# A diffusion block's opening: another order of loads, one unit beside the modulations, one behind them, and filler matmuls

## The chip, the cores and the metric

The kernel runs on one core of one Trainium2 chip. The metric is the device time of one execution in microseconds (us), the median of the runs shown. Activations lie transposed in the core: 128 partitions hold features, the free axis holds the tokens. There are 256 latent tokens (LAT) and 256 context tokens (CTX), so a row of both is 512 columns wide, and 1024 features are eight chunks of 128, called k below.

## The reference, cut to what matters

The model has two layers. Each layer computes nine modulation vectors per stream from a conditioning vector, then an FFN branch, a mixer and a second FFN branch. Only the start of the first layer matters here:

```python
mod  = split(silu(c)     @ ada_w[0] + ada_b[0], 9)
modc = split(silu(c_ctx) @ ada_w[0] + ada_b[0], 9)

def ffn_branch(h, g, shift, scale, gate, w13, w2):
    a = rmsnorm(h, g) * (1.0 + scale) + shift
    g_, up = split(a @ w13, 2)
    return 0.5 * gate * ((silu(g_) * up) @ w2)

h  = h  + ffn_branch(h,  norm_g[0, 0], mod[0],  mod[1],  mod[2],  ffn_w13[0, 0], ffn_w2[0, 0])
hc = hc + ffn_branch(hc, norm_g[0, 0], modc[0], modc[1], modc[2], ffn_w13[0, 0], ffn_w2[0, 0])
```

The first product with w13 needs the normed and modulated activations, and these need shift and scale of both streams, that is 8 MB of ada_w, and the mean squares of both streams.

## The kernel before

**Precision.** A product of float32 is made of three matmuls. An operand is split into a high part in the chip's fp32r type and a low part, the difference: a_h and a_l for activations, wh and wl for weights, g_h and g_l for the FFN's inner activations. `mm3` issues wh by a_h, wh by a_l and wl by a_h for each chunk k.

**Units.** The weights come in units of 1 MB, a pair of 128-column blocks: for w13 one gate block and one up block. `Units.fetch` issues the load on SP's queue into a raw tile (two buffers), `Units.load` splits it: ScalarE copies to wh, VectorE subtracts to wl, once per block. wh and wl have five buffers each. `units.get` hands a unit out and loads the next. A whole unit of w13 takes 48 matmuls of 512 columns: two blocks, eight chunks, three matmuls.

**Modulations.** For the first norm the shifts and scales are computed on TensorE in four quads of 1 MB twice (`quad_load`, kh 0 and 1). `quad_sum` runs 16 small matmuls for each half (32 rows in the profile, since a float32 matmul shows as two rows), which add into a PSUM tile gt. `quad_end` copies gt to gs on VectorE (L118), transposes it on TensorE (L119) and makes mod (L122) and gain (L124) on VectorE for two chunks k. Quad q serves the chunks 2q and 2q+1.

**Norm.** `rstd_diag` sums squares over the partitions with matmuls (st), makes the mean (L244), takes the power -1/2 on GpSimd (L246) and builds diagonal matrices (L249). `rstd_rows` broadcasts them with a matmul (bc). `norm_k` makes for one chunk and one stream u on VectorE (L261), a_h on ScalarE (L264) and a_l on VectorE (L265). u has three buffers.

**Opening.** `first` loads, in the program's order, quad 0, unit 0, quad 1, unit 1, quads 2 and 3; all `adaq` tiles share four buffers, so quads 2 and 3 wait until quad 0's and 1's sums have read theirs. The squares of h (L997, L999, L1003), 20 warming matmuls on ones into a tile called warm, the statistics, quad 0 and the first two norms follow. `pair` then computes units 0 and 1 together: for chunks 0 to 5 it issues both units' matmuls of the chunk and calls the hook ahead of chunks 0, 2 and 4, which sums quads 1, 2 and 3 and makes their norms; chunks 6 and 7 close the two units, and `glu` makes g_h and g_l. Then unit 2 and the rest follow, one unit after the other.

**What sets the order.** The tile framework plans the order of each engine's instructions itself, by the program's order and by when it expects operands and buffers. Three things bind it: data and buffer dependences; `keep_in_program_order`, which `MM` uses while the list `in_order` holds something, so that these TensorE instructions keep the order of the program; and `issue_after(ins)`, which puts the instructions traced in its block behind `ins` on the engine of `ins` alone. Before, the pinned stretch ends ahead of quad 0's end; the order of the tiles and sums behind it is the planner's. All large loads go through SP's queue, four small ones through ScalarE's.

Of the kernel before, what the change touches and what calls it, by code (L numbers as in the profile page):

```python
# [10 lines left out]
F32 = mybir.dt.float32  # L11
F32R = mybir.dt.float32r
# [37 lines left out]
def hybrid_block(ctx: ExitStack, tc: tile.TileContext, h_in, s_in, s_row, ada0, ada, ada_b, norm_g, final_g,  # L50
# [17 lines left out]
    def ps_t(shape, name):  # L68
        return ps.tile(shape, F32, tag="t", name=name, bufs=2)
# [1 line left out]
    h = big.tile([P, KD, NT], F32, name="h")  # L71
    a_h = Rows(big.tile([P, KD * NT + P], F32R, name="a_h"))
    a_l = Rows(big.tile([P, KD * NT + P], F32R, name="a_l"))
    g_h = big.tile([P, KD, NT], F32R, name="g_h")
    g_l = big.tile([P, KD, NT], F32R, name="g_l")
    A = (a_h, a_l)
    GG = (g_h, g_l)

    sv = const.tile([P, KD, 32], F32, name="sv")
    nc.scalar.dma_start(out=sv, in_=s_in)  # L80
    for hf in BOTH:
        nc.sync.dma_start(out=h[:, :, HALF[hf]], in_=h_in[hf])
    ab = const.tile([P, 2, 9, KD, 2], F32, name="ab")
    nc.scalar.dma_start(out=ab, in_=ada_b)
    ng = const.tile([P, 2, 3, KD, 2], F32, name="ng")
# [16 lines left out]
    def quad_load(pool, q):  # L102
        us = []
        for kh in range(2):
            u = pool.tile([P, 4, 512], F32, tag="adaw", name=f"adaq{q}_{kh}", bufs=4)
            nc.sync.dma_start(out=u, in_=ada0[q, kh])
            us.append(u)
        return us

    def quad_sum(gt, kh, u):  # L110
        for kc in range(4):
# [4 lines left out]
    def quad_end(pool, gt, q):  # L116
        gs = pool.tile([P, P], F32, tag="gs", name=f"gs{q}", bufs=2)
        V.tensor_copy(out=gs, in_=gt[:, 0, :])  # L118
        T.transpose(out=gt[:, 1, :], in_=gs, identity=ident)  # L119
        k = slice(2 * q, 2 * q + 2)  # L120
        src = gt[:, 1, :].rearrange("p (k m c) -> p k m c", k=2, m=2)[:, :, :, 0:2]
        V.tensor_tensor(out=mod[0][:, 0:2, k, :].rearrange("p m k r -> p k m r"), in0=src,  # L122
                        in1=ab[:, 0, 0:2, k, :].rearrange("p m k r -> p k m r"), op=ALU.add)
        V.scalar_tensor_tensor(out=gain[0][:, 0, k, :], in0=mod[0][:, 1, k, :], scalar=1.0, in1=ng[:, 0, 0, k, :],  # L124
                               op0=ALU.add, op1=ALU.mult)
# [131 lines left out]
    def norm_k(li, n, hf, bc, k):  # L257
        tag = f"n{li}_{n}_{hf}_{k}"
        sh = mod[li][:, 3 * n, k, hf:hf + 1]
        u = tmp.tile([P, NL], F32, tag="u", name=f"u_{tag}", bufs=3)  # L260
        V.scalar_tensor_tensor(out=u, in0=h[:, k, HALF[hf]], scalar=gain[li][:, n, k, hf:hf + 1], in1=bc,  # L261
                               op0=ALU.mult, op1=ALU.mult)
        ah = a_h[:, k, HALF[hf]]
        S.activation(out=ah, in_=u, func=AF.Identity, bias=sh)  # L264
        V.scalar_tensor_tensor(out=a_l[:, k, HALF[hf]], in0=u, scalar=sh, in1=ah.bitcast(F32),  # L265
                               op0=ALU.add, op1=ALU.subtract)

    def norm_begin(li, n, hf):
        dg = rstd_diag(ssq[hf], D, f"n{li}_{n}_{hf}")
# [98 lines left out]
    def ffn(li, fi, halves, items, nxt, first=None):  # L368
# [3 lines left out]
        with tc.tile_pool(name=f"ffn{f}", bufs=2) as fp:  # L372
# [20 lines left out]
            def pair(ws, cols, nm, nouter, hook=None):  # L393
# [9 lines left out]
                for j in range(2):  # L403
                    for x in range(2):
                        mm3(accs[j][x], ws[j][x], A, range(nouter, KD), cols, first=(nouter == 0))
                    glu(accs[j][0], accs[j][1], j, cols, f"{tag}_{j}_{nm}")

            def raw_glu(pg, pu, j, bc, nm):

                sh = fp.tile([P, 2], F32, tag="sh", name=f"sh_{nm}")  # L410
                ts = []
                for x, pp in enumerate((pg, pu)):
                    V.tensor_copy(out=sh[:, x:x + 1], in_=pp[:, NL:NL + 1])
                    ts.append(fp.tile([P, NL], F32, tag=f"t{x}", name=f"t{x}_{nm}"))
# [24 lines left out]
            if len(halves) == 1:  # L439
                bc = raw_pair()  # L440
            elif first:
                hook = first(fp)
                ws = [units.get(f"{tag}u{j}") for j in range(2)]
                pair(ws, slice(0, NT), "a", 6, hook)
# [4 lines left out]
            if prep:  # L449
                prep()  # L450
            slot()
            slot()
# [532 lines left out]
    ffn_units(3, (LAT,))  # L985

    def first(fp):
        qs = [quad_load(fp, 0)]
        pins = units.load()
        qs.append(quad_load(fp, 1))  # L990
        units.load()
        qs += [quad_load(fp, 2), quad_load(fp, 3)]
        for hf in BOTH:
            sq = []
            for x in range(4):
                sq.append(fp.tile([P, 2, NL], F32, tag="sg" if x < 2 else "gg", name=f"sq_{hf}_{x}"))
                S.activation(out=sq[x], in_=h[:, 2 * x:2 * x + 2, HALF[hf]], func=AF.Square)  # L997
                if x % 2:
                    V.tensor_tensor(out=sq[x - 1], in0=sq[x - 1], in1=sq[x], op=ALU.add)  # L999
            ssq[hf] = [tmp.tile([P, NL], F32, tag=f"ssq{hf}", name=f"ssq{hf}_in", bufs=1),  # L1000
                       tmp.tile([P, NL], F32, tag="sq", name=f"sq{hf}_in", bufs=2)]
            for x in range(2):
                V.tensor_tensor(out=ssq[hf][x], in0=sq[0][:, x, :], in1=sq[2][:, x, :], op=ALU.add)  # L1003
        gt = ps_t([P, 2, P], "gt0")
        wm = acc([P, NT], "warm")
        in_order.append(1)
        for _ in range(20):
            MM(wm[:, 0:P], ones, ones, start=True, stop=True)
        dgs = [rstd_diag(ssq[LAT], D, "n0_0_0")]
        quad_sum(gt, 0, qs[0][0])  # L1010
        bcs = [rstd_rows(dgs[0], "n0_0_0")]
        dgs.append(rstd_diag(ssq[CTX], D, "n0_0_1"))
        quad_sum(gt, 1, qs[0][1])
        bcs.append(rstd_rows(dgs[1], "n0_0_1"))
        in_order.clear()
        quad_end(fp, gt, 0)

        def norms(q):
            if q:
                gt = ps_t([P, 2, P], f"gt{q}")  # L1020
                for kh in range(2):
                    quad_sum(gt, kh, qs[q][kh])
                quad_end(fp, gt, q)
            for k in (2 * q, 2 * q + 1):
                for hf in BOTH:
                    norm_k(0, 0, hf, bcs[hf], k)
        with tc.issue_after(pins[0].ins), tc.issue_after(pins[1].ins):
            norms(0)
        return lambda k: norms(k // 2 + 1) if k in (0, 2, 4) else None

    ffn(0, 0, BOTH, [(0, m, kp, 2) for m in range(2, 8) for kp in range(4)], (0, 1), first)
    na_layer(0)
# [111 lines left out]
```

## Time and profile before

| | us |
|---|---|
| median of 3 runs | 1791.26 |
| lowest, highest | 1790.46, 1792.51 |
| profiled execution | 1788.52 |
| its span, first to last instruction | 1786.4 |
| TensorE busy in it | 1761.5 |
| granted TensorE clock, mean | 0.995 |

The span is one execution seen by the hardware profiler; the execution's own time holds 2.1 us more around it. A granted clock of 1.00 is 2.4 GHz and one of 0.50 is 1.2 GHz. In the rows PE is TensorE, PEld its weight loads, DVE VectorE, ACT ScalarE, POOL GpSimd, and SPq the queue of SP. A row that says "x3" merges three instructions in a row, and its second number runs from the start of the first to the end of the last.

### The profile page before, as it was taken

Reading aid. Unit: us, or ns where it says so; the run is one execution under the profiler, and the core shown is the slowest. Engines: PE = TensorE matmul, PEld = TensorE weight load, DVE = VectorE, ACT = ScalarE, POOL = GpSimd, SP = SyncE. Lnnn points to the kernel's source line nnn. Section 1 sums busy time; section 2 is a strip of 40 time slices with the busy share of each in tenths; the row PEclk is TensorE's granted clock in tenths of the full one; section 3 lists DMA queues with packets and bytes.
Section 4 is the critical chain, followed back from the end, with each engine's and each line's share of the span. In section 5 each row is a group of like instructions: output and inputs, shape, how many; then the busy total and the mean of one; then the engine's idle time right before and its main releaser. Section 6 shows DMA issues by size and latency. Waiting matters only on the chain.

```text
span 1786.4 us, 24670 instructions
## 1 busy us (share of the span) xinstructions
PE 1761.5 (99%) x9920; PEld 1520.3 (85%) x9920; DVE 1181.2 (66%) x2042; ACT 699.5 (39%) x1074; POOL 23.4 (1%) x42
## 2 busy tenths in 40 slices
PE   7999999999999999999999999999999999999998
PEld 6888888897777798888888988888889988999997
DVE  4897777366678778877773666553335776677665
ACT  3422213235455543222223332221223856654443
POOL 0000000000000000000000000000000000000000
PEclk8999999999999999999999999999999999999999
DMA  9665552322131235645543255532222422245542
GB/s 388 229 234 185 196 189 94 105 97 101 36 113 65 81 118 194 230 165 190 195 153 145 95 181 212 196 142 94 95 94 95 154 71 72 95 160 195 177 180 93
DMA packets 42834, 263.70 MB, mean 148 GB/s; under 512 B 4960, under 2 KB 7392, under 8 KB 13152
## 3 DMA queue, kind: packets, MB, share of 16 engines
q1 hardware_dynamic: 40128, 257.97, 39.6%
q10 hardware_dynamic: 2592, 4.16, 0.8%
q8 instruction: 78, 1.28, 0.3%
q14 instruction: 36, 0.29, 0.0%
HBM read 261.06 MB, written 1.05 MB: 147 GB/s over the span
## 4 chain that ended last, share of the span: by engine, by line
PE 96%; ACT 1%; DVE 1%; DMA 1%; issue 0%; POOL 0%; SPq 0%; POOLq 0%; DVEq 0%; ACTq 0%
PE pu_f L200 22%; PE pg_f L200 22%; PE po_f2g L200 5%; PE po_f0g L200 5%; PE po_f1g L200 5%; PE pkq L200 5%; PE po_f3g L200 4%; PE nav_p L200 2%; PE mlv_p L200 2%; PE mpk L200 2%; PE pat L200 1%; PE sp L200 1%; PE mpq L200 1%; PE po_mlwo L200 1%; PE po_nao L200 1%; PE mpo L200 1%
## 5 line engine op out<-in xcount | busy, mean ns | idle before, releaser
L140 DVE SCALAR_TENSOR_TENSOR jk<-ada,sb 128x1024 f32<-128x1024 f32 x224 | 273.6, 1221 | 3.5
L388 DVE TENSOR_TENSOR gg_f<-sg_f,pu_f 128x512 f32<-128x512 f32 x60 | 41.2, 687 | 154.7 <-PE pu_f L200 154.7
L180 ACT ACTIVATE wh_f2u<-raw_f2u 128x1024 fp32r<-128x1024 f32 x44 | 46.7, 1062 | 148.2 <-PE pg_f L200 55.3
L180 ACT ACTIVATE wh_f1u<-raw_f1u 128x1024 fp32r<-128x1024 f32 x44 | 46.7, 1062 | 142.4 <-PE pg_f L200 51.8
L180 ACT ACTIVATE wh_f0u<-raw_f0u 128x1024 fp32r<-128x1024 f32 x44 | 46.4, 1060 | 135.2 <-PE pg_f L200 50.3
L181 DVE TENSOR_TENSOR wl_f2u<-raw_f2u,wh_f2u 128x1024 fp32r<-128x1024 f32 x44 | 53.9, 1224 | 39.0 <-ACT wh_f2u L180 37.8
L180 ACT ACTIVATE wh_f3u<-raw_f3u 128x1024 fp32r<-128x1024 f32 x44 | 46.1, 1058 | 48.5 <-PE pg_f L200 15.9
L181 DVE TENSOR_TENSOR wl_f1u<-raw_f1u,wh_f1u 128x1024 fp32r<-128x1024 f32 x44 | 53.8, 1224 | 16.3 <-ACT wh_f1u L180 15.2
L181 DVE TENSOR_TENSOR wl_f0u<-raw_f0u,wh_f0u 128x1024 fp32r<-128x1024 f32 x44 | 53.7, 1223 | 15.0 <-ACT wh_f0u L180 14.0
L181 DVE TENSOR_TENSOR wl_f3u<-raw_f3u,wh_f3u 128x1024 fp32r<-128x1024 f32 x44 | 53.4, 1222 | 13.5 <-ACT wh_f3u L180 13.4
L200 PE MATMUL pg_f<-a_h,wh_f1u 128*128 128x512 f32 x160 | 62.3, 389 | 0.0
L200 PE MATMUL pg_f<-a_h,wh_f2u 128*128 128x512 f32 x160 | 62.3, 389 | 0.0
L200 PE MATMUL pg_f<-a_l,wh_f1u 128*128 128x512 f32 x160 | 62.3, 389 | 0.0
L200 PE MATMUL pg_f<-a_l,wh_f2u 128*128 128x512 f32 x160 | 62.3, 389 | 0.0
L200 PE MATMUL pg_f<-a_h,wh_f0u 128*128 128x512 f32 x160 | 62.2, 389 | 0.0
L200 PE MATMUL pg_f<-a_l,wh_f0u 128*128 128x512 f32 x160 | 62.2, 389 | 0.0
L200 PE MATMUL pg_f<-a_h,wl_f0u 128*128 128x512 f32 x160 | 62.2, 389 | 0.0
L200 PE MATMUL pu_f<-a_h,wh_f0u 128*128 128x512 f32 x160 | 62.2, 389 | 0.0
L200 PE MATMUL pu_f<-a_l,wh_f0u 128*128 128x512 f32 x160 | 62.2, 389 | 0.0
L200 PE MATMUL pu_f<-a_h,wl_f0u 128*128 128x512 f32 x160 | 62.2, 389 | 0.0
L200 PE MATMUL pg_f<-a_h,wl_f1u 128*128 128x512 f32 x160 | 62.2, 389 | 0.0
L200 PE MATMUL pu_f<-a_h,wh_f1u 128*128 128x512 f32 x160 | 62.2, 389 | 0.0
(509 smaller groups left out, 5617.4 us busy)
## 6 DMA issues: line engine op xcount, KB each, us to landing
ada<-in_ada SPq DMA_DIRECT2D x64, 1024.0 KB, 5.6
raw_f0u<-in_w SPq DMA_DIRECT2D x22, 1024.0 KB, 4.9
raw_f1u<-in_w SPq DMA_DIRECT2D x22, 1024.0 KB, 4.9
raw_f2u<-in_w SPq DMA_DIRECT2D x22, 1024.0 KB, 4.8
raw_f3u<-in_w SPq DMA_DIRECT2D x22, 1024.0 KB, 4.8
adaq<-in_ada SPq DMA_DIRECT2D x8, 1024.0 KB, 12.4
raw_f0g<-in_w SPq DMA_DIRECT2D x8, 1024.0 KB, 4.8
raw_kq<-in_na_kq SPq DMA_DIRECT2D x8, 1024.0 KB, 4.8
```

The source lines that it names most:

```text
L140: V.scalar_tensor_tensor(out=junk, in0=u[:, j, :], scalar=1.0, in1=sb[:, r, :], op0=ALU.mult, op1=ALU.mult, accum_out=mod[li][:, m, 2 * kp ...
L180: pins = (S.activation(out=wh[:, :n], in_=raw[:, i, :n], func=AF.Copy), V.tensor_tensor(out=wl[:, :n], in0=raw[:, i, :n], in1=wh[:, :n].bi ...
L181: V.tensor_tensor(out=wl[:, :n], in0=raw[:, i, :n], in1=wh[:, :n].bitcast(F32), op=ALU.subtract))
L200: ins = T.matmul(*args, **kw)
L388: V.tensor_tensor(out=gg, in0=sg, in1=pu, op=ALU.mult)
```

## The change

The second half of h is loaded behind unit 0's weights, and unit 0 is loaded right behind the first half. The quads follow in order, unit 1's load comes last. Quads 2 and 3 are loaded into the space that g_h and g_l will have, so they need no buffer of quads 0 and 1; g_h and g_l are allocated when the last norms have been issued.

The LAT statistics are put behind unit 0's split on VectorE. The warming matmuls become 29, and further ones of the same kind (`idle`) stand at fixed places: 13 behind the LAT statistics, 3 behind quad 0's second sum, 4 behind the CTX broadcast, 4 behind quad 1's end. The order of TensorE stays pinned to the end of the opening, transposes too.

`first_pair` replaces `pair`: unit 0's chunk 0, quad 1's first sum, chunk 1, quad 1's second sum and end, fillers; then for quads 2 and 3 a sum, a chunk, a sum, the end, a chunk; then chunks 6 and 7 and unit 0's `glu`. Unit 1 is split behind the last norm on ScalarE and VectorE and runs its 48 matmuls in one piece. The load of the row of c (`prep`) is made behind this, its ScalarE instruction behind the last norm's.

```diff
     sv = const.tile([P, KD, 32], F32, name="sv")
     nc.scalar.dma_start(out=sv, in_=s_in)
-    for hf in BOTH:
-        nc.sync.dma_start(out=h[:, :, HALF[hf]], in_=h_in[hf])
+    nc.sync.dma_start(out=h[:, :, HALF[LAT]], in_=h_in[LAT])
...
+    def quad_load(pool, q, kh):
+        if q < 2:
             u = pool.tile([P, 4, 512], F32, tag="adaw", name=f"adaq{q}_{kh}", bufs=4)
-            nc.sync.dma_start(out=u, in_=ada0[q, kh])
-            us.append(u)
-        return us
+        elif kh == 0:
+            u = big.tile([P, 8, 512], F32, tag=f"g{q - 2}", name=f"adaq{q}")
+            g_place[q] = u
+            u = u[:, 0:4, :]
+        else:
+            u = g_place[q][:, 4:8, :]
+        nc.sync.dma_start(out=u, in_=ada0[q, kh])
+        return u
...
-        T.transpose(out=gt[:, 1, :], in_=gs, identity=ident)
+        tc.keep_in_program_order(T.transpose(out=gt[:, 1, :], in_=gs, identity=ident))
...
+            def first_pair(norms, idle):
+                w = units.get(f"{tag}u0", False)
+                accs = [[acc([P, NT], f"p{x}_{tag}_{j}_a") for x in "gu"] for j in range(2)]
+                def tile_k(k):
+                    for x in range(2):
+                        mm3(accs[0][x], w[x], A, [k], slice(0, NT), first=(k == 0), last=(k == KD - 1))
+                tile_k(0)
+                norms(1, 0)
+                tile_k(1)
+                norms(1, 1)
+                norms(1, 2)
+                idle(4)
+                for q in (1, 2):
+                    norms(q + 1, 0)
+                    tile_k(2 * q)
+                    norms(q + 1, 1)
+                    pins = norms(q + 1, 2)
+                    tile_k(2 * q + 1)
+                tile_k(KD - 2)
+                tile_k(KD - 1)
+                glu(accs[0][0], accs[0][1], 0, slice(0, NT), f"{tag}_0_a")
+                with tc.issue_after(pins[0].ins), tc.issue_after(pins[1].ins):
+                    units.load()
+                w = units.get(f"{tag}u1")
+                for x in range(2):
+                    mm3(accs[1][x], w[x], A, range(KD), slice(0, NT))
+                glu(accs[1][0], accs[1][1], 1, slice(0, NT), f"{tag}_1_a")
+                in_order.clear()
+                return pins
...
     def first(fp):
-        qs = [quad_load(fp, 0)]
         pins = units.load()
-        qs.append(quad_load(fp, 1))
-        units.load()
-        qs += [quad_load(fp, 2), quad_load(fp, 3)]
+        nc.sync.dma_start(out=h[:, :, HALF[CTX]], in_=h_in[CTX])
+        qs = [[quad_load(fp, 0, kh) for kh in range(2)]]
+        for q in range(1, 4):
+            qs.append([quad_load(fp, q, kh) for kh in range(2)])
+        units.fetch()
...
-        for _ in range(20):
-            MM(wm[:, 0:P], ones, ones, start=True, stop=True)
-        dgs = [rstd_diag(ssq[LAT], D, "n0_0_0")]
+
+        def idle(n):
+            for _ in range(n):
+                MM(wm[:, 0:P], ones, ones, start=True, stop=True)
+        idle(29)
+        with tc.issue_after(pins[1].ins):
+            dgs = [rstd_diag(ssq[LAT], D, "n0_0_0")]
+        idle(13)
         quad_sum(gt, 0, qs[0][0])
         bcs = [rstd_rows(dgs[0], "n0_0_0")]
         dgs.append(rstd_diag(ssq[CTX], D, "n0_0_1"))
         quad_sum(gt, 1, qs[0][1])
+        idle(3)
+        quad_end(fp, gt, 0)
         bcs.append(rstd_rows(dgs[1], "n0_0_1"))
-        in_order.clear()
-        quad_end(fp, gt, 0)
+        idle(4)
...
-        with tc.issue_after(pins[0].ins), tc.issue_after(pins[1].ins):
-            norms(0)
-        return lambda k: norms(k // 2 + 1) if k in (0, 2, 4) else None
+        norms(0, 2)
+        return norms, idle
```

In the new kernel `norms(q, 0)` and `norms(q, 1)` are the two sums of quad q, and `norms(q, 2)` is its end with the four norms of its two chunks.

## Rows read from the trace of the kernel before

**Rows 1.** The page: busy time of TensorE, its share of the span, instructions.
```profile
PE 1761.5 (99%) x9920; PEld 1520.3 (85%) x9920; DVE 1181.2 (66%) x2042; ACT 699.5 (39%) x1074; POOL 23.4 (1%) x42
```

**Rows 2.** Table by stages: stage, length, TensorE busy (instructions), clock, DMA, GB/s.
```profile
50.00:100.00 50.00, 50.00 (x223) 1.00 0.64 234
```

**Rows 3.** Chain of waits behind the opening: start, length, what.
```profile
56.16 5.44 PE pg_f L200 x24
```

**Rows 4.** Timeline of TensorE, third unit: start, length, engine, line, operation.
```profile
55.99 0.39 PE L200 MATMUL pg_f<-a_h,wh_f0u 128*128 128x512 f32 x1
```

**Rows 5.** Timeline, first work that waited for loads; idle time before it in brackets.
```profile
10.19 2.19 ACT L997 ACTIVATE sq<-h 128x512 f32<-128x512 f32 x4 [1.04 <-DMA h<-in_h_in]
...
17.58 2.00 ACT L180 ACTIVATE wh_f0u<-raw_f0u 128x1024 fp32r<-128x1024 f32 x2 [5.21 <-DMA raw_f0u<-in_w]
...
21.38 1.08 PE L200 MATMUL gt<-adaq,sv 128*32 128x128 f32 x32 [2.46 <-DMA adaq<-in_ada]
```

**Rows 6.** Table by stages: busy PE, PEld, DVE, ACT, POOL; clock; DMA; GB/s.
```profile
16.00:19.00 3.00, 2.38 (x41) 1.73 (x40) 0.89 (x5) 1.42 (x2) 0.69 (x1) 1.00 1.02 421
22.00:29.50 7.50, 6.97 (x62) 4.60 (x52) 4.02 (x12) 1.87 (x5) 0.00 (x0) 0.54 1.01 422
```

**Rows 7.** Timeline: quad 0's end, the first norms and the first tile.
```profile
17.97 0.28 DVE L118 COPY gs<-gt 128x128 f32<-128x128 f32 x1
...
18.64 0.27 PE L119 MATMUL gt<-ident,gs 128*128 128x128 f32 x1
...
19.24 2.36 DVE L181 TENSOR_TENSOR wl_f0u<-raw_f0u,wh_f0u 128x1024 fp32r<-128x1024 f32 x2
...
21.51 1.26 DVE L261 SCALAR_TENSOR_TENSOR u_n<-h,gain,bc_n 128x256 f32<-128x256 f32 x3
...
22.99 0.80 PE L200 MATMUL pg_f_a<-a_h,wh_f0u 128*128 128x512 f32 x1 [0.53 <-ACT a_h L264]
...
23.62 0.79 PE L200 MATMUL pg_f_a<-a_l,wh_f0u 128*128 128x512 f32 x1
...
24.93 0.48 DVE L265 SCALAR_TENSOR_TENSOR a_l<-u_n,mod,a_h 128x256 fp32r<-128x256 f32 x1 [0.58 <-ACT a_h L264]
```

**Rows 8.** Timeline: second sum of quad 2, its end and the next norms.
```profile
36.54 0.40 PE L200 MATMUL pg_f_a<-a_h,wl_f0u 128*128 128x512 f32 x1
...
36.87 1.08 PE L200 MATMUL gt<-adaq,sv 128*32 128x128 f32 x32
37.88 0.50 PE L200 MATMUL pu_f_a<-a_h,wh_f0u 128*128 128x512 f32 x1
...
38.01 0.29 DVE L118 COPY gs<-gt 128x128 f32<-128x128 f32 x1 [3.45 <-PE gt L200]
38.21 0.40 PE L200 MATMUL pu_f_a<-a_l,wh_f0u 128*128 128x512 f32 x1
...
38.68 0.27 PE L119 MATMUL gt<-ident,gs 128*128 128x128 f32 x1
...
38.99 0.17 DVE L122 TENSOR_TENSOR mod<-gt,ab 128x8 f32<-128x8 f32 x1 [0.69 <-PE gt L119]
...
39.39 1.26 DVE L261 SCALAR_TENSOR_TENSOR u_n<-h,gain,bc_n 128x256 f32<-128x256 f32 x3
```

**Rows 9.** SP's queue: issue of the last four quad loads; the last one's time to landing.
```profile
14.71 12.38 SPq L106 DMA_DIRECT2D adaq<-in_ada  x4
...
adaq<-in_ada SPq DMA_DIRECT2D x1, 1024.0 KB, 9.4
```

**Rows 10.** Warming matmuls in two stages; last statistics matmul; the power on GpSimd.
```profile
1.05:5.00 3.95, 3.95 (x18) 1.00 0.77 228
5.00:7.83 2.83, 2.83 (x24) 1.00 1.12 355
...
11.19 0.36 PE L200 MATMUL st_n<-ones,sq_in 128*128 128x1 f32 x2
...
11.84 0.71 POOL L246 TENSOR_TENSOR rs_n<-ms_n,mhalf 128x2 f32<-128x2 f32 x1 [10.53 <-DVE ms_n L244]
```

More of the change, by code (lines that the diff above doesn't have):

```diff
@@ L73, in hybrid_block @@
     a_l = Rows(big.tile([P, KD * NT + P], F32R, name="a_l"))
-    g_h = big.tile([P, KD, NT], F32R, name="g_h")
-    g_l = big.tile([P, KD, NT], F32R, name="g_l")
     A = (a_h, a_l)
-    GG = (g_h, g_l)
+    g_h = g_l = GG = None
     sv = const.tile([P, KD, 32], F32, name="sv")
     nc.scalar.dma_start(out=sv, in_=s_in)
-    for hf in BOTH:
-        nc.sync.dma_start(out=h[:, :, HALF[hf]], in_=h_in[hf])
+    nc.sync.dma_start(out=h[:, :, HALF[LAT]], in_=h_in[LAT])
     ab = const.tile([P, 2, 9, KD, 2], F32, name="ab")
@@ L100, in hybrid_block, with g_tiles @@
     gain = [const.tile([P, 3, KD, 2], F32, name=f"gain{i}") for i in range(2)]
-    def quad_load(pool, q):
-        us = []
-        for kh in range(2):
+    def quad_load(pool, q, kh):
+        if q < 2:
             u = pool.tile([P, 4, 512], F32, tag="adaw", name=f"adaq{q}_{kh}", bufs=4)
-            nc.sync.dma_start(out=u, in_=ada0[q, kh])
-            us.append(u)
-        return us
+        elif kh == 0:
[6 more added lines that the diff above has]
+        return u
+    g_place = {}
+    def g_tiles():
+        nonlocal g_h, g_l, GG
+        g_h = big.tile([P, KD, NT], F32R, tag="g0", name="g_h")
+        g_l = big.tile([P, KD, NT], F32R, tag="g1", name="g_l")
+        GG = (g_h, g_l)
     def quad_sum(gt, kh, u):
@@ L263, in norm_k @@
         ah = a_h[:, k, HALF[hf]]
-        S.activation(out=ah, in_=u, func=AF.Identity, bias=sh)
-        V.scalar_tensor_tensor(out=a_l[:, k, HALF[hf]], in0=u, scalar=sh, in1=ah.bitcast(F32),
-                               op0=ALU.add, op1=ALU.subtract)
+        hi = S.activation(out=ah, in_=u, func=AF.Identity, bias=sh)
+        return hi, V.scalar_tensor_tensor(out=a_l[:, k, HALF[hf]], in0=u, scalar=sh, in1=ah.bitcast(F32),
+                                          op0=ALU.add, op1=ALU.subtract)
     def norm_begin(li, n, hf):
@@ L441, in ffn @@
             elif first:
-                hook = first(fp)
-                ws = [units.get(f"{tag}u{j}") for j in range(2)]
-                pair(ws, slice(0, NT), "a", 6, hook)
+                pins = first_pair(*first(fp))
             else:
@@ L448, in ffn @@
                 pair(ws, HALF[CTX], "c", 0)
-            if prep:
+            if first:
+                with tc.issue_after(pins[0].ins):
+                    prep()
+            elif prep:
                 prep()
@@ L1013, in first, with norms @@
         quad_sum(gt, 1, qs[0][1])
+        idle(3)
+        quad_end(fp, gt, 0)
         bcs.append(rstd_rows(dgs[1], "n0_0_1"))
-        in_order.clear()
-        quad_end(fp, gt, 0)
-        def norms(q):
+        idle(4)
+        gts = {}
+        def norms(q, step):
+            if step < 2:
+                if step == 0:
+                    gts[q] = ps_t([P, 2, P], f"gt{q}")
+                quad_sum(gts[q], step, qs[q][step])
+                return
             if q:
[L1020 to L1023, printed above, removed]
+                quad_end(fp, gts[q], q)
             for k in (2 * q, 2 * q + 1):
                 for hf in BOTH:
-                    norm_k(0, 0, hf, bcs[hf], k)
-        with tc.issue_after(pins[0].ins), tc.issue_after(pins[1].ins):
-            norms(0)
-        return lambda k: norms(k // 2 + 1) if k in (0, 2, 4) else None
+                    pins = norm_k(0, 0, hf, bcs[hf], k)
+            if q == 3:
+                g_tiles()
+            return pins
+        norms(0, 2)
+        return norms, idle
     ffn(0, 0, BOTH, [(0, m, kp, 2) for m in range(2, 8) for kp in range(4)], (0, 1), first)
```

## Prediction, before the changed kernel ran

> **What bounds the kernel now.** I read the page first: TensorE is busy for 1761.5 of 1786.4 us [rows 1], so a microsecond can only be won where it stands idle or slow. The table by stages says where: from 50 us on a 50 us stage shows 50.00 us busy at clock 1.00 [rows 2], and the chain of waits walks there through 24 matmuls in 5.44 us, that is 0.227 us for each matmul of 512 columns [rows 3]. Only the opening is loose. I call its end the start of the third unit's first matmul, 55.99 us in this trace [rows 4]. What lies behind it is the same work in both kernels and is already dense there, so the change is worth what it moves this point.
>
> The two units that the change reorders have 96 matmuls, 96 x 0.227 = 21.8 us. In the timeline the first of them starts at 22.99 [rows 7], so the stretch to 55.99 is 33.0 us long and holds 11.2 us of something else. Six sums of modulations lie in it. One costs the stream 1.22 us: the matmul before starts at 36.54, the sum at 36.87, the next matmuls at 37.88 and 38.21 [rows 8], so 1.01 us for its 32 rows and 0.21 us because two spacings are 0.33 instead of 0.227. Six are 7.3 us. The granted clock explains most of the rest: its mean from 22.0 to 29.5 is 0.54 [rows 6], which is the lower level, 1.2 GHz, for 0.92 of it, 6.9 us; the tile begins about 0.6 us into that, and what TensorE then did lost half of 6.3 us, 3.2 us. Before the fall TensorE had been idle from 18.9 to 21.4, where a sum waited 2.46 us for its load [rows 5]. The last 0.7 us are small waits.
>
> **The change part by part.** *Loads.* In the timeline the waits on loads give the landings: the second slot at 10.19, the fifth at 17.58, the sixth at 21.3 [rows 5]; the last modulation load, twelfth, is issued at 26.8 and takes 9.4 us, 36.2 [rows 9]. That is 2.5 us for each 1 MB slot with one longer step. All of them are 1 MB, so a new order permutes the slots. The first unit's weights go from the fifth slot to the second, h's second half from second to third, quad 0 from third and fourth to fourth and fifth, quad 1 keeps its slots, quads 2 and 3 gain one, and the second unit's weights go from the eighth to the twelfth, 36.2 at latest. In before SP held the four loads of quads 2 and 3 from 14.71 to 27.1 for their buffers [rows 9]; in g's space they wait for none. This removes no bytes and what is queued behind them on SP (third unit, rows of c, ada items) moves by one slot at most; none of it is wanted before 45 us. I price that at nothing. If the cover were gone, one late slot would cost 2.5 us.
>
> *Start of the first tile.* Before, VectorE spent 2.36 us from 19.24 on the second half of the first unit's split, and only then, at 21.51, made u of the first norm, whose gain it had made before [rows 7]. With the weights in the second slot, ScalarE's two copies (2.00 us [rows 5]) and VectorE's two subtractions (2.36 us) end near 10.2 + 1.0 + 2.4 = 13.7. The LAT statistics are put behind them on VectorE: the pow (0.71 us), the diagonals and the row broadcast [rows 10] are done by about 15.5, and the first sum's load lands at 15.1, a slot ahead of 17.58; the broadcast follows that sum, so this wait is hidden. The second sum starts with its load, slot five, at 17.7 and ends 1.08 us later [rows 8], at 18.8. Then three fillers, the copy (0.29), transpose (0.27), mod and gain. The copy starts 0.06 after a sum's end (37.95 to 38.01), mod 0.31 after the transpose and u 0.40 after mod [rows 8]. From copy to transpose it was 0.67, 17.97 to 18.64 [rows 7], with a broadcast's weight load in between; I take 0.57. Sum's end to u is then 0.06 + 0.57 + 0.31 + 0.40 = 1.34, and 1.45 with the fillers ahead of the transpose. From u to the first matmul 1.48, to the second, which needs a_l, 2.11 [rows 7]. First tile at 18.8 + 1.45 + 1.48 = 21.75: 1.25 us earlier than 22.99.
>
> *Fillers.* A call is two rows. From 1.05 to 5.00 there are 18 rows and from 5.00 to 7.83 there are 24 [rows 10], 40 in all with those that stand in both: 0.44 us a call first, then 0.24. Those that are added run behind a busy stretch; I take 0.24 and keep 0.44 as the upper end. 29 calls end at 7.83 + 9 x 0.24 = 10.0 (11.8); the 8 matmuls of the statistics, whose last row ended at 11.55 before [rows 10], come next; 13 more calls end at 14.7 (18.7). Only the upper end would push the second sum, to about 21.5: 0 to 2.7 us, I take 0, since the first sum's load lands at 15.1. The four in the middle of the run cost 0.96 (1.76).
>
> *The fixed order.* Here the change adds waits. Before, the planner put other matmuls between a sum and its transpose: the second sum of quad 2 ends at 37.95 and its transpose stands at 38.68 behind three matmuls, without a stall [rows 8]. Pinned directly behind its sum, a transpose waits for the copy, and every matmul behind it waits too: the next can start 0.06 + 0.57 + 0.04 = 0.67 after the sum's end and not at once. Three of these fall in the run, 2.0 us. Further, tile 0 and tile 2 have nothing else to issue while the second matmul waits for a_l (2.11 - 1.48 - 0.23 = 0.4 each).
>
> *The end of the run.* After the last sum, call its end E, TensorE has the transpose and tile 5, to E + 2.05; tile 6 can start at E + 1.34 + 1.48 = E + 2.8 and its second matmul at E + 3.45; tile 7's two at E + 1.34 + 3.4 and + 3.95 (the fourth a_l starts at 24.93, just behind its a_h, and ends at 25.41, against 21.51) [rows 7], so it ends issuing at E + 6.4. The second unit's split is put behind the last norm on ScalarE and VectorE: its first subtraction ends about E + 7.1 (1.0 and 1.2 us for half the rows' 2.00 and 2.36), and the third matmul of the unit waits 0.25 for it. Then 46 x 0.227 = 10.43, to E + 17.55.
>
> *Sum.* With M = 21.75 for the first tile: two tiles, two sums and a wait for a_l, 2.72 + 2.44 + 0.4 = 5.56, to the end of quad 1's sums; from there to the end of quad 2's a transpose 0.67, fillers 0.96, one tile 1.36, two sums 2.44 and 0.4: 5.83; to E a transpose, two tiles and two sums: 5.83; then 17.55. 21.75 + 5.56 + 5.83 + 5.83 + 17.55 = 56.52, against 55.99: 0.5 us later. In words: 1.25 us of earlier start, 3.2 us of clock and 0.7 us of small waits are won; 2.0 us of transposes, 0.96 us of fillers and 2.7 us of norm latency (0.4, 0.4 and 1.9 at the end) are paid. By the landings, no load binds after the first tile: the last sum's load, now eleventh and by 36.2 at latest, stands against a sum that the order reaches near 37.8.
>
> The profiled execution took 1788.52 us, span 1786.4 and 2.1 around it, 2.7 under the median 1791.26 of the three runs. I add the shift to the median: 1791.26 + 0.5 = 1791.8 us.
>
> The Trainium skill, page TensorE: Matmul & The Clock Gate, section Step-by-step: what each phase is for, says that of what waits at TensorE only weight loads are pulled ahead and matmuls stay in program order. It speaks against pinning the transposes. In the timeline no matmul overtakes another either [rows 8], but no row has a stalled transpose with matmuls behind it; if they could overtake, the three stalls would go and the sum would be 2.0 us lower.
>
> **The rivals.** *The order costs nothing* (0.14). The copy, the norm and a_l might come earlier or the stream absorb them, so that only the gains remain: 1.25 + 3.2 + 0.7 less 0.96 for fillers, 4.2 us: 1787.1. For it: the copy starts 0.06 after its sum [rows 8]. Against it: the 0.67 is a chain of measured pieces.
>
> *The fillers do not hold the clock* (0.16). TensorE has from 18.8 to 21.75 only seven fillers, 1.7 us, a transpose of 0.27 us and a broadcast. If the clock falls there as it did near 22.4 and stays for as long, 6.9 us, half of it is lost again: 56.5 + 3.4 = 59.9, 3.9 later: 1795.2, slower. It decides once the granted clock reads 0.50 for over 6.2 us after 18 (0.5 + half of 6.2 = 3.6). For it: in before the low level outlasted sums and tiles from 23 to 29. Against it: from 16 to 19 TensorE was busy for 2.38 of 3 us and the clock read 1.00 [rows 6].
>
> *The third unit's split gets in front* (0.18). It isn't put behind a norm. Before, ScalarE and VectorE took one copy and one subtraction of it between the norms; placed before the last two norms it costs up to 1.0 + 1.2 = 2.2 us (half of the two-block runs [rows 5, 7]): about 1793.5, still within the bound, beyond it only with another loss (0.04).
>
> *It does not do what it says*: the unpinned engines might be laid out as before, u behind other VectorE work; the first tile then starts near 23 and the sum is 1.25 us later, 1793. I count it with the forecast (together 0.52).
>
> **How the numbers follow.** A change of 0.2%, 3.6 us, is about what a measurement of this kernel can tell from none. Faster: the first rival, 0.14. Slower: the clock 0.16 and the split's tail 0.04, 0.20. Within: 0.66. The range goes down to the first rival, of which 1786.8 leaves out about half, and up past the clock to 1796.
>
> **What would show it.** In the trace after: first tile near 21.75; clock 1.00 from 5 us on; a gap of about 0.5 us before each pinned transpose; waits of tiles 6 and 7 on u and a_l; third unit near 56.5. It is wrong if the tiles run without those gaps, if the third unit starts before 52.8 or after 59.6, or if the later stages shift.

## The result, and the profile after

| | before | after |
|---|---|---|
| median of 6 runs, us | 1790.81 | 1799.46 |
| lowest, highest | 1789.35, 1792.51 | 1798.55, 1800.51 |
| profiled execution | 1788.52 | 1799.23 |
| its span | 1786.4 | 1797.4 |
| mean granted clock | 0.995 | 0.996 |

The ratio is 1.0051, with a 95% interval from 1.004 to 1.0061: 8.7 us slower. 1791.8 us had been predicted, with a range from 1786.8 to 1796.0.

The page after, the row that answers to [rows 1]:

```profile
PE 1772.1 (99%) x9986; PEld 1526.3 (85%) x9986; DVE 1182.6 (66%) x2042; ACT 701.6 (39%) x1076; POOL 25.2 (1%) x42
```

TensorE's share is 99% as before, so the share hides the loss. The opening is read first. Table by stages of after, columns as in [rows 6]:

```profile
16.00:19.00 3.00, 3.00 (x67) 2.54 (x55) 0.87 (x3) 0.00 (x0) 0.70 (x1) 1.00 1.01 421
22.00:29.50 7.50, 6.89 (x93) 4.95 (x97) 3.12 (x10) 0.99 (x4) 0.00 (x0) 1.00 1.02 419
29.50:40.00 10.50, 9.53 (x149) 6.63 (x142) 7.00 (x20) 3.56 (x8) 0.00 (x0) 1.00 1.01 418
40.00:57.00 17.00, 16.32 (x68) 12.32 (x67) 9.59 (x17) 10.09 (x13) 0.00 (x0) 1.00 0.81 320
```

The stretch that ran at 0.54 before [rows 6] now has 1.00. Timeline of TensorE in after, the first tile, a pinned transpose, tile 6 and the third unit, which answer to [rows 7], [rows 8] and [rows 4]; in brackets the idle time before a row and what ended it:

```profile
22.06 0.49 PE L210 MATMUL pg_f_a<-a_h,wh_f0u 128*128 128x512 f32 x1 [0.58 <-ACT a_h L274]
...
26.65 1.08 PE L210 MATMUL gt<-adaq,sv 128*32 128x128 f32 x32
28.15 0.33 PE L129 MATMUL gt<-ident,gs 128*128 128x128 f32 x1 [0.41 <-DVE gs L128]
28.31 1.06 PE L210 MATMUL warm<-ones 128*128 128x128 f32 x8
...
41.85 0.50 PE L210 MATMUL pg_f_a<-a_h,wh_f0u 128*128 128x512 f32 x1 [0.54 <-ACT a_h L274]
...
56.60 0.39 PE L210 MATMUL pg_f<-a_h,wh_f0u 128*128 128x512 f32 x1
```

The third unit starts at 56.60; the sum had said 56.52. So the opening is 0.6 us later than before and explains 0.6 of 11.0 us of span. The profiled execution of before took 2.3 us less than its median and that of after 0.2 less, so about 2 of these 11.0 us are the choice of execution and not the change. The others are found by asking of later tiles when their first or last matmul starts in either trace; "last" is the start of the last product with wh and g_h. NA and ML are the mixers of the first and the second layer:

| matmul | before | after | later by |
|---|---|---|---|
| third unit, first | 55.99 | 56.60 | 0.6 |
| NA, first (nav_p) | 395.6 | 396.2 | 0.6 |
| NA, last of its output (po_nao) | 626.9 | 629.8 | 2.9 |
| ML, first of its output gate (mpo) | 1398.5 | 1400.6 | 2.1 |
| ML, first of its keys (mpk) | 1421.3 | 1428.1 | 6.8 |
| ML, last of its output (po_mlwo) | 1583.1 | 1591.8 | 8.7 |
| last FFN branch, last (po_f3g) | 1775.5 | 1786.0 | 10.5 |

The FFN branches ahead of NA and between the mixers add nothing (0.8 comes back between them). The loss is made in the mixers, 2.3 us in NA and 6.6 in ML; the last branch adds 1.8. The waits of TensorE over the whole span, the longest of before and then of after (us in total, times, longest):

```profile
PE gt L200 <- DMA adaq<-in_ada: 3.6, 2, 2.5
PE tpx L859 <- DVE xx L849: 2.6, 1, 2.6
...
PE pat L200 <- ACT pt L662: 2.1, 4, 0.5
```

```profile
PE tpx L902 <- DVE xx L892: 3.4, 1, 3.4
PE mpo L210 <- DVE wl_mlo L191: 3.2, 1, 3.2
...
PE pat L210 <- ACT pt L705: 0.6, 1, 0.6
```

The opening's wait for a load is gone from the list's head, and a wait of 3.2 us for a split unit of weights (wl_mlo, in ML) is new. In NA no wait for weights shows: the waits of its attention (pat) are even shorter, the clock reads 1.00 in both traces, and TensorE's matmuls stand in another order. What NA's 2.3 us consist of stays open.

Where the wait for wl_mlo comes from, in the timelines of SP's queue and VectorE, the load and the first subtraction of that unit, before and then after:

```profile
1379.07 0.33 SPq L167 DMA_DIRECT2D raw_mlo<-in_ml_og  x1
1390.40 1.21 DVE L181 TENSOR_TENSOR wl_mlo<-raw_mlo,wh_mlo 128x1024 fp32r<-128x1024 f32 x1
```

```profile
1387.49 0.33 SPq L177 DMA_DIRECT2D raw_mlo<-in_ml_og  x1
1403.13 1.22 DVE L191 TENSOR_TENSOR wl_mlo<-raw_mlo,wh_mlo 128x1024 fp32r<-128x1024 f32 x1
```

Before, the unit was split 8.1 us ahead of its first matmul (1398.5 less 1390.40). After, it is loaded 8.4 and split 12.7 us later, 2.5 us behind that first matmul (1400.6), which can run because wh alone serves it. Table by stages there, before and then after:

```profile
1400.00:1410.00 10.00, 10.00 (x85) 9.95 (x84) 9.80 (x18) 8.35 (x16) 0.00 (x0) 1.00 0.15 52
...
1430.00:1440.00 10.00, 7.39 (x53) 6.79 (x51) 9.67 (x18) 2.27 (x3) 0.00 (x0) 1.00 0.30 107
1440.00:1450.00 10.00, 9.99 (x70) 9.26 (x71) 5.80 (x11) 8.74 (x11) 0.00 (x0) 1.00 0.00 1
```

```profile
1400.00:1410.00 10.00, 6.84 (x46) 6.64 (x45) 9.80 (x19) 6.67 (x13) 0.00 (x0) 0.83 0.24 71
...
1430.00:1440.00 10.00, 10.00 (x50) 8.44 (x49) 7.41 (x11) 5.49 (x6) 0.21 (x1) 1.00 0.33 134
1440.00:1450.00 10.00, 6.59 (x43) 6.27 (x42) 7.03 (x13) 6.26 (x9) 0.00 (x0) 0.83 0.27 105
```

From 1400 to 1410 TensorE loses 3.2 us, the wait for wl_mlo, and the granted clock falls behind it. The wait between 1440 and 1450 (tpx) is not new: before, it stands between 1430 and 1440 and lasts 2.6 us at clock 1.00; after, it lasts 3.4, and the clock falls behind it. So the two waits explain 3.2 + 0.8 = 4.0 of ML's 6.6 us. A clock of 0.83 over 10 us is 3.4 us at the lower level, twice here; if half of it is lost, as an estimate, this is up to 1.7 us each time and enough for the rest.

The line that does it stands in the diff. Before, `first` called `units.load()` twice, for units 0 and 1, and each `units.get` loaded one more: the kernel ran **two units ahead** of what it used. After, `first` loads unit 0 and only fetches unit 1 (the raw load, no split), `units.get(f"{tag}u0", False)` hands unit 0 out without loading another, and unit 1 is loaded behind the last norms. From there it is **one unit ahead**. That lasts to the last output unit of ML. `out_proj` hands that one out without loading another, in both kernels, and since `get` loads a unit that is missing, both run the last FFN branch one ahead; only its first unit is split later in after (1592.81 against 1578.88). In NA two of the value units are handed out without a load, which follows a little later: in between before is one ahead and after none.

### The profile page after: what moved, and what is told of

It is laid out like the page before. It is cut to its first block, busy times and chain, and to the rows that moved or that the text cites. A ratio compares the mean times of both kernels' runs of the same rounds, so it can differ in the third digit from the quotient of the medians.

```text
span 1797.4 us, 24789 instructions
## 1 busy us (share of the span) xinstructions
PE 1772.1 (99%) x9986; PEld 1526.3 (85%) x9986; DVE 1182.6 (66%) x2042; ACT 701.6 (39%) x1076; POOL 25.2 (1%) x42
## 4 chain that ended last, share of the span: by engine, by line
PE 95%; DVE 2%; ACT 1%; DMA 1%; issue 0%; SPq 0%; POOL 0%; POOLq 0%; DVEq 0%; ACTq 0%
PE pu_f L210 22%; PE pg_f L210 22%; PE po_f2g L210 5%; PE po_f0g L210 5%; PE po_f1g L210 5%; PE pkq L210 4%; PE po_f3g L210 4%; PE mlv_p L210 3%; PE nav_p L210 2%; PE mpk L210 2%; PE pat L210 2%; PE mpo L210 1%; PE po_nao L210 1%; PE sp L210 1%; PE po_mlwo L210 1%; PE tp L699 1%
## 5 line engine op out<-in xcount | busy, mean ns | idle before, releaser
L210 PE MATMUL pu_f<-a_l,wh_f1u 128*128 128x512 f32 x160 | 62.2, 389 | 0.0
L210 PE MATMUL pu_f<-a_h,wl_f1u 128*128 128x512 f32 x160 | 62.2, 389 | 0.0
```

## The experiments

The theory: the loss behind the opening is the missing unit of lead, and the opening itself is worth what the prediction said. The first rival: what the change did to the opening lives on (another order on the queues, g_h and g_l in other places, a row of c loaded later) and the mixers suffer from that; then more lead brings nothing. The second: only the first mixer or only the opening needs the lead. A third stands in the expectations as the planner theory: any other plan of the tile framework costs something by chance. Each kernel was timed beside the kernel before on the same chip, the groups on different chips. The ratio isn't the quotient of the two medians (0.9991 for e1), and the runs of one kernel spread over 2 to 6 us, so a single microsecond between two rows tells nothing by itself; "third unit" and the tiles are as in the table above, all in us.

| kernel | median (before beside it) | ratio, 95% interval | third unit | po_nao | mpk | po_mlwo | po_f3g |
|---|---|---|---|---|---|---|---|
| e1_two_ahead | 1789.17 (1790.81) | 0.9999 [0.999, 1.0008] | 56.38 | 627.3 | 1421.7 | 1583.4 | 1776.0 |
| e2_one_ahead | 1799.89 (1790.81) | 1.0053 [1.004, 1.0065] | 57.33 | 630.5 | 1428.9 | 1592.8 | 1787.1 |
| e5_two_from_ml | 1793.83 (1790.81) | 1.0018 [1.0009, 1.0027] | 56.41 | 629.5 | 1424.8 | 1586.5 | 1779.1 |
| e6_two_from_na | 1790.35 (1790.81) | 0.9998 [0.9989, 1.0006] | 56.49 | 627.3 | 1421.7 | 1585.0 | 1777.7 |
| e3_no_fillers | 1794.87 (1790.6) | 1.0025 [1.0016, 1.0034] | 60.80 | 631.7 | 1426.1 | 1587.8 | 1780.6 |
| e4_loads_only | 1790.64 (1790.6) | 1.0001 [0.9992, 1.001] | 58.01 | 628.9 | 1423.3 | 1586.5 | 1779.0 |
| e7_cover | 1787.39 (1790.6) | 0.9984 [0.9975, 0.9993] | 54.45 | 625.3 | 1420.6 | 1582.3 | 1774.7 |
| e8_three_ahead | 1793.6 (1790.6) | 1.002 [1.0011, 1.0029] | 54.59 | 625.6 | 1424.5 | 1588.3 | 1780.4 |
| e10_more_fillers | 1790.14 (1791.12) | 0.9993 [0.9984, 1.0002] | 58.20 | 629.0 | 1424.3 | 1587.6 | 1780.0 |
| e11_34_22 | 1789.57 (1790.61) | 0.9996 [0.9987, 1.0004] | 55.42 | 626.3 | 1420.6 | 1582.4 | 1775.2 |
| e12_29_22 | 1791.1 (1790.61) | 1.0001 [0.9992, 1.001] | 54.89 | 625.8 | 1420.1 | 1584.0 | 1776.6 |

### The lead alone, given back: e1_two_ahead

```diff
                 w = units.get(f"{tag}u1")
+                units.load()
                 for x in range(2):
```

> The changed kernel with one more unit split ahead behind the second unit's hand-out, so that units run two ahead of their use again. Depth theory (the change left the weights one unit ahead instead of two for the whole kernel): the opening still ends near 56.6 us, the later stages fall back, total 0.5 to 0.7 us above before, near 1791.4. Opening theory (the new opening leaves a backlog of loads or VectorE work that the mixers pay for later): total stays near 1799. Planner theory (any new opening reshuffles the plan by chance): anything between, with no reason to come back to before.

One more load behind the opening, all else as after: 10.3 us come back (1799.46 to 1789.17), 9.3 by the ratios. Its waits, the longest:

```profile
PE tpx L903 <- DVE xx L893: 2.6, 1, 2.6
PE pat L210 <- ACT pt L706: 2.1, 4, 0.5
```

The wait for wl_mlo is gone and tpx is back at 2.6, as before. The first rival falls: order, places and late row of c are all still there.

### The lead alone, taken away: e2_one_ahead

```diff
-                ws = [units.get(f"{tag}u{j}") for j in range(2)]
+                ws = [units.get(f"{tag}u{j}", j == 1) for j in range(2)]
```

> The kernel before with its own opening, but the first unit handed out without splitting the next, so that units run one ahead from there on. Depth theory: 6 to 10 us above before, near 1799, with the first output gate tile of the second mixer waiting about 3 us for its low weights as in the changed kernel. Opening theory: the opening is the old one, so within 1 us of before. Planner theory: a shift of either sign.

The kernel before, with one load less ahead, takes 1799.89, 9.1 us more, without a word of the change in it, and shows the same two waits:

```profile
PE tpx L859 <- DVE xx L849: 3.4, 1, 3.4
PE mpo L200 <- DVE wl_mlo L181: 3.2, 1, 3.2
```

So the lead is enough for the loss, and e1 shows that nothing else is needed. The third unit is 1.3 us later in this trace than in that of before; its clock reads 0.50 from 16 to 19 us, where [rows 6] has 1.00, so this need not be the edit's doing.

### Where the lead is needed: e5_two_from_ml, e6_two_from_na

```diff
+    units.load()
     na_layer(0)
```

That is e6; e5 has the same line ahead of `ml_layer(1)`.

> The changed kernel with the second unit of lead put back only ahead of the second layer's mixer. Depth theory: the 2 us that the first mixer lost stay, the 6.5 us of the second mixer and the 1.6 us of the FFN behind it come back: about 3 us above before, near 1794. Opening theory: near 1799. Planner theory: no forecast.

> The changed kernel with the second unit of lead put back ahead of the first layer's mixer, behind the whole first FFN. Depth theory: the first FFN hides one unit of lead, so all of the later loss comes back: about 0.6 us above before, near 1791.4. Opening theory: near 1799.

With the extra load from NA on, everything comes back (1790.35), so the FFN branch ahead of it doesn't need the second unit: a unit of w13 lasts 10.9 us there (two rows as in [rows 3]). With it from ML on, the time is 1793.83: 5.6 of 8.7 us come back, po_nao stays at 629.5. The two mixers share the loss, and the second rival falls. e1, e2, e5 and e6 all came out within 2.3 us of what the lead alone forecasts, which chance would hardly do four times; that the lead acts through another plan, in NA above all, isn't excluded.

### The fillers: e3_no_fillers

```diff
-        idle(29)
+        idle(20)
...
-        idle(13)
+        idle(0)
...
-        idle(3)
+        idle(0)
...
-        idle(4)
+        idle(0)
...
-                idle(4)
+                idle(0)
```

> The changed kernel, two units ahead, with 20 warming matmuls at the start and no other fillers. If the fillers hold the clock: it reads 0.50 for 3.4 to 7 us between 12 and 30, the third unit starts 1 to 3 us later than 56.6, total 1792 to 1794. If they are not needed: clock 1.00, third unit near 55.6, the total 1 us lower than with them.

This is e1 with the 20 warming matmuls of before and no others. The third unit comes 4.4 us later than in e1 (60.80 against 56.38) and the time is 5.7 us longer. Table by stages:

```profile
12.00:16.00 4.00, 0.64 (x13) 0.67 (x17) 3.14 (x8) 2.19 (x4) 0.70 (x1) 0.67 1.00 415
16.00:23.00 7.00, 6.50 (x72) 5.27 (x61) 1.69 (x7) 0.00 (x0) 0.70 (x1) 0.50 1.02 421
34.00:37.00 3.00, 3.00 (x25) 2.00 (x28) 0.92 (x3) 0.51 (x1) 0.00 (x0) 0.50 1.02 415
```

TensorE is busy for 0.64 of the 4 us ahead of the first sum's load, and the clock then reads 0.50 for 7 us, and again at 34; in e1 it reads 1.00 in all three stages. The fillers do hold it, and leaving them out costs more than the 1 to 3 us forecast.

### The loads alone: e4_loads_only

```diff
-    for hf in BOTH:
-        nc.sync.dma_start(out=h[:, :, HALF[hf]], in_=h_in[hf])
+    nc.sync.dma_start(out=h[:, :, HALF[LAT]], in_=h_in[LAT])
...
-        qs = [quad_load(fp, 0)]
         pins = units.load()
+        nc.sync.dma_start(out=h[:, :, HALF[CTX]], in_=h_in[CTX])
+        qs = [quad_load(fp, 0)]
```

> The kernel before with the new order of the first loads alone: first unit's weights second, h's second half third. The split no longer stands in front of the first norm, so the first tile starts 1 to 1.3 us earlier than 22.99; the clock falls as before; third unit 0.5 to 1.3 us earlier than 55.99, total near 1790.

The kernel before with the new order of its first loads. The time is that of before, but the opening was forecast wrong: the third unit is 2.0 us later in the trace, not earlier. By how much the opening changed the traces can't say, since e4's profiled execution lies 1.2 us above its median and that of before 2.3 under its own. The first sum waits 3.75 us for its load and the low clock from 16 to 23 then covers all of quad 0. Here a better order of loads, without work that keeps TensorE running up to them, only moved the fall to another place.

### A version with two ahead and the transposes covered: e7_cover

```diff
-                norms(1, 2)
-                idle(4)
-                for q in (1, 2):
-                    norms(q + 1, 0)
-                    tile_k(2 * q)
-                    norms(q + 1, 1)
-                    pins = norms(q + 1, 2)
-                    tile_k(2 * q + 1)
+                pins = norms(1, 2)
+                norms(2, 0)
+                norms(2, 1)
+                tile_k(2)
+                pins = norms(2, 2)
+                tile_k(3)
+                with tc.issue_after(pins[0].ins), tc.issue_after(pins[1].ins):
+                    units.load()
+                norms(3, 0)
+                tile_k(4)
+                norms(3, 1)
+                tile_k(5)
+                pins = norms(3, 2)
+                w1 = units.get(f"{tag}u1", False)
+                for k in range(KD - 2):
+                    tile1_k(k)
                 tile_k(KD - 2)
                 tile_k(KD - 1)
...
                 with tc.issue_after(pins[0].ins), tc.issue_after(pins[1].ins):
                     units.load()
-                w = units.get(f"{tag}u1")
-                for x in range(2):
-                    mm3(accs[1][x], w[x], A, range(KD), slice(0, NT))
+                    units.load()
+                tile1_k(KD - 2)
+                tile1_k(KD - 1)
```

`tile1_k` is `tile_k` for unit 1, whose load moves ahead of quad 3's.

> Two units ahead again, the new loads and the fillers ahead of the first tile kept, and the opening's order changed: the sums of quad 2 stand behind quad 1's transpose in place of the four fillers, the other transposes stand behind a tile, the second unit's weights are loaded ahead of quad 3 and split behind quad 2's norms, and its chunks 0 to 5 stand between the last norm's sums and the first unit's chunks 6 and 7. If the stalls of the pinned transposes and of the last norms are what eats the opening's gain: third unit near 52.6 us against 56.0 before, total near 1787.4, 3.4 below before. If other waits take their place: third unit at 55 to 56.5, total within 1 us of before.

Quad 2's sums take the place of four fillers, a tile stands ahead of its transpose and of quad 3's, and unit 1's chunks stand between the last sums and the tiles that wait for them. 1787.39 us, 0.9984 of before [0.9975, 0.9993]: faster than both kernels. The third unit came at 54.45 and not at 52.6. The clock fell ahead of the first tile; whether this cost anything is asked of e10 to e12. Table by stages:

```profile
10.00:12.00 2.00, 1.65 (x11) 1.61 (x12) 1.94 (x4) 1.60 (x2) 0.00 (x0) 0.87 1.17 379
12.00:14.00 2.00, 2.00 (x12) 2.00 (x11) 1.18 (x3) 1.33 (x3) 0.70 (x1) 0.50 0.98 407
14.00:16.00 2.00, 2.00 (x15) 1.96 (x14) 1.97 (x5) 0.86 (x2) 0.00 (x0) 0.78 1.01 422
```

### More lead still: e8_three_ahead

```diff
                 with tc.issue_after(pins[0].ins), tc.issue_after(pins[1].ins):
                     units.load()
                     units.load()
+                units.load()
                 tile1_k(KD - 2)
```

Unlike the two above it, the third load isn't put behind the last norm.

> The same with a third unit of lead. The split tiles have room for two and a half units. If lead alone decides the mixers: as with two or up to 2 us less. If two is what the buffers can use: the same as with two within 1 us, although the plan of the later stages is another one. If any other plan of these stages costs (planner theory): several us more.

Three units ahead cost 6.2 us against two (1793.6 against 1787.39). Both forecasts of the lead theory missed (up to 2 us less, or the same within 1), and "several us more" was the planner theory's. Table by stages in ML, e7 and then e8:

```profile
1400.00:1410.00 10.00, 9.30 (x78) 9.10 (x77) 9.64 (x18) 8.46 (x16) 0.00 (x0) 1.00 0.22 64
```

```profile
1400.00:1410.00 10.00, 8.56 (x70) 8.38 (x70) 10.00 (x23) 9.06 (x17) 0.00 (x0) 1.00 0.24 69
```

The waits of e8 that e7 has not or has shorter (tpx 2.6 us there):

```profile
PE tpx L914 <- DVE xx L904: 3.5, 1, 3.5
...
PE mpq L210 <- DVE cy_q L794: 1.1, 1, 1.1
...
PE mpo L210 <- DVE cy_q L794: 0.8, 1, 0.8
```

VectorE is busy for the whole 10.00 us, 9.64 in e7, and TensorE waits not for weights but for the mixer's own vector work (cy_q, xx). That splits of a further unit stand in front of it fits the rows; it wasn't tested by itself, and another plan by chance isn't excluded.

### How many fillers: e10_more_fillers, e11_34_22, e12_29_22

```diff
-        idle(29)
+        idle(34)
...
-        idle(13)
+        idle(22)
```

That is e11, on e7; e10 has the first edit alone, e12 the second alone.

> The kernel of the covered opening (two units ahead), with 34 fillers ahead of the statistics in place of 29. In its trace with 29 the fillers ended at 9.50, TensorE stood still for 0.85 us, and the granted clock read 0.87, 0.50 and 0.78 in the three stages from 10 to 16 us; its first tile came at 22.62 instead of 22.06 and its second sum started at 18.50. If that fall of the clock is what the gap cost, five more calls (0.24 us each, 1.2 us, to 10.7) close the gap, the clock reads 1.00 from 8 to 22, the first tile comes 0.5 to 0.9 us earlier (21.7 to 22.1), the third unit at 53.6 to 54.0 instead of 54.45, and the time is near 1786.7. Rival: the first tile is set by the load of quad 0's second half and the vector engines, not by the clock; then it stays near 22.6, the third unit near 54.5 and the time near 1787.4.

> The covered opening with 34 fillers ahead of the statistics and 22, in place of 13, behind them. With 34 and 13 the second batch ran out at 14.50, the first sum's load came only at 16.85 (it was 2.39 us of idle time), the granted clock read 0.92 and 0.50 from 16 to 24 and the first tile came at 26.35. If that idle time is the cause, 9 more calls of 0.24 us (to about 16.7) bridge it: no idle time of over 1 us ahead of the first sum, clock 1.00 from 4 to 24, first tile at 22.4 to 22.8, third unit at 54.2 to 54.6, time 1786.8 to 1787.8. Rival: the added fillers are themselves the loss (they push the sums and the first tile back whatever the clock does): then the first tile is later than 23 and the time is 1789 or more, at clock 1.00.

> The covered opening with 29 fillers ahead of the statistics and 22 behind them. The gap of 0.85 us ahead of the statistics stays. If that gap brings the clock down as in the kernel with 29 and 13 (0.87, 0.50, 0.78 from 10 to 16), 22 calls at 0.44 us each last longer than the load needs, some 4 us more than 13 would by the slow part: the first sum starts 1.5 to 2.5 us later than 16.1, and the time is 1 to 2.5 us above that of 34 and 22. If the clock holds, the two are alike within 0.5 us.

Timeline of e10 at the first sum:

```profile
11.35 3.15 PE L210 MATMUL warm<-ones 128*128 128x128 f32 x26
16.89 1.24 PE L210 MATMUL gt<-adaq,sv 128*32 128x128 f32 x32 [2.39 <-DMA adaq<-in_ada]
```

and its table by stages:

```profile
18.00:24.00 6.00, 6.00 (x52) 5.26 (x49) 0.93 (x4) 0.00 (x0) 0.69 (x1) 0.50 1.01 421
```

The clock held through the fillers, so these ended at 14.50, the load came at 16.9, and the clock fell behind the 2.39 us of waiting: first tile at 26.35, third unit at 58.20. In e7 the 13 calls had run at the low clock for a part (4.78 instead of 3.15 us) and so lasted until the load: the slow stretch bridged the gap. With 22 calls (e11) the wait is 0.37 and the clock reads 1.00 from 8 to 28, as expected, but the load still landed at 17.0, the first tile came at 23.55, and the median is 1789.57: the signs of the rival (later than 23, 1789 or more). In e12 the clock read 1.00 from 8 to 28 too, and its third unit came 0.5 us earlier than in e11 (54.89 against 55.42); yet its median is 1.5 us higher, with intervals that overlap. So it isn't shown that the fall of the clock kept e7 from 52.6: with the clock at 1.00, and more fillers, the third unit came no earlier.

Nor do these traces differ in the opening alone. The wait for xx (tpx), far behind it in ML, is 2.6 us long in e1 and in e6. Table by stages behind it, e1 and then e6:

```profile
1440.00:1450.00 10.00, 9.65 (x69) 8.96 (x70) 5.80 (x11) 8.40 (x11) 0.00 (x0) 1.00 0.01 2
```

```profile
1440.00:1450.00 10.00, 9.61 (x62) 9.21 (x63) 4.30 (x10) 6.87 (x10) 0.00 (x0) 0.83 0.01 2
```

The same wait, and the clock falls behind it in one execution and not in the other. From mpk to po_mlwo e1 takes 161.7 us, e6 163.3. By the table above e4, e10 and, with a wait of 3.3 us, e12 are of e6's kind there (163.2 to 163.9), before, e3, e5, e7 and e11 of e1's (161.7 to 161.8). So some 1.5 us of the span hang on this one place, whatever the opening does. The profiled execution of e10 (1792.64) lies 2.5 us above its median, that of e11 (1787.96) is the lowest of its runs, so neither need stand for the others. By the medians e7 is 2.2 to 3.7 us faster than its variants, but its interval overlaps each of theirs.

In the traces of after, e1, e5 and e6 the first sum started between 15.30 and 15.52, in e10 and e11 at 16.89 and 17.01. Why the load comes later in these is open, and with it whether e7's opening is better than theirs.

## Why the prediction was wrong, step by step

**What it was wrong about.** The step that failed is its first conclusion: "What lies behind it is the same work in both kernels and is already dense there, so the change is worth what it moves this point." The work is the same, but when its weights are split is not. Under *Loads* the third unit and what follows it "moves by one slot at most" and was priced "at nothing". The third unit is even issued earlier (by 18.3 us, before not until 27.2), and nothing waits for it; the fourth is issued at 47.1, before by 33.7. What the term left out is the number of units split ahead, which the opening sets for all that follows up to ML's output and which fell from two to one. That costs 9.1 us by itself (e2) and 10.3 by e1. "Dense" was read from the one 50 us stage of [rows 2], an FFN branch; the mixers were not looked at. In ML VectorE is busy for 9.80 of 10 us before too, so a split that comes late finds little room. "If the later stages shift" stood among the signs that would prove it wrong, and that is what happened. A slower kernel had been given 0.20, but through the clock and the third unit's split, and neither came.

**What the reader could have done.** The diff shows two `units.load()` in `first` before; after, there is one `load` and one `fetch` in it, a second `load` in `first_pair`, and a `get` with `False`. When unit 1 is handed out, units 2 and 3 have been loaded in the one, unit 2 alone in the other. The rival would have been: the lead drops by one; it can decide where a unit lasts shorter than load and split need; its price there is a wait for the late unit plus the clock behind it. ML's output gate shows this: its unit is 48 matmuls of 256 columns, 0.12 us apart in the timeline, 5.8 us. NA, whose units have 48 matmuls of 512 columns as in the FFN, would not have been found this way.

**The opening was right.** By its own steps, each against e1 or after:

- First tile: 21.75 predicted, 22.06 in after; 1.25 us earlier was 0.93. The first sum's load was put at 15.1 and came at 15.5.
- The clock: 1.00 throughout, as forecast. e3 prices the fillers at 4.4 us in the opening. The rival "the fillers do not hold the clock", which has the fillers in place, had 59.9 for the third unit; without fillers it is 60.80.
- The pinned transposes: TensorE waits 0.41 us ahead of each of three (28.15, 33.86, 39.61). The quads' sums end, by the copy behind them, near 27.74, 33.46 and 39.20, and the next matmul behind the transpose starts 0.57, 0.49 and 0.49 later, 1.6 us in all where 2.0 was forecast. The sum had 27.31, 33.14 and 38.97 for these ends: each stage took 5.7, where 5.83 was forecast.
- The run's end: 17.55 forecast from the last sum to the third unit, 17.4 measured (56.60 less 39.20); tile 6 waits 0.54 for its a_h.
- The sum: 56.52 against 56.60. So close is luck in part: the steps are off by up to 0.3 us and cancel. One addition is wrong and carries nothing (10.2 + 1.0 + 2.4 is 13.6, not 13.7). With the lead restored, the same opening takes 1789.17 us, 0.9999 of before: the forecast of no measurable change for the opening holds.

The Trainium skill, page TensorE: Matmul & The Clock Gate, section Step-by-step: what each phase is for, says that matmuls stay in program order and only weight loads are pulled ahead. The trace agrees: at each of the three transposes TensorE stood still for 0.41 us with eight filler rows or a tile queued behind it.

**The rivals.** "The third unit's split gets in front" and "it does not do what it says" did not happen: from 27.8 to 44.74 VectorE has no subtraction of a split, the first (u1's) follows the last norm, and the tiles start where the sum has them. "The order costs nothing" did not either, in this order; e7 shows that the order can be made to cost less, 54.45.

## What to carry to other kernels

When an edit touches the first use of a prefetching helper, count how many blocks are loaded ahead at the end of the edited part, before and after: that number lasts until other code sets it again, and it can be paid far from the edit. Read every kind of stage, those with short blocks first, before calling what lies behind "the same work". More lead is not always better: two were better than one by 9 to 10 us and, in one comparison, better than three by 6.

## What the runs showed of the hardware

- Filler matmuls last as long as the clock lets them: 13 calls took 3.15 us at 1.00 (e10) and 4.78 in a stretch that read 0.87, 0.50 and 0.78 (e7). A fixed count therefore bridges a wait at the low clock and leaves a gap at the high one.
- A gap's length alone did not decide whether the clock fell. Ahead of the statistics after waited 1.2 us and kept 1.00; e7 waited 0.85 us at the same place and fell to 0.50. In ML the clock read 1.00 behind a wait of 2.6 us in e1 and 0.83 behind the same wait in e6, 1.6 us of time apart.
- The first sum's load, at the same place in the queue, came between 15.3 and 17.0 us in the eight traces of the new order where TensorE waited for it.
